# Strassen operand sums of the gate and FFN stages formed in earlier stages and kept in DRAM, one plain pair less in each stage, in a hybrid mixer layer on one core

## The chip, the core and the metric

The kernel runs on one core of a Trainium2 chip. A core has a matrix engine (TensorE, here PE), a vector engine (VectorE, DVE), a scalar engine (ScalarE, ACT), a general engine (GpSimd, POOL), a sync engine (SyncE, SP) that issues most of the transfers, and 16 DMA engines that move data between device memory (DRAM) and the on-chip memory (SBUF); matmul results land in a second on-chip memory, PSUM. Each engine runs its own instructions strictly in program order and waits for others by semaphores. The metric is the device time of one execution in microseconds (us), the median of several runs.

## The reference

One layer (batch 1, 1024 tokens, width 1024, all float32). Cut to what matters here:

```python
u = rms_norm(x, norm_mix_pre)
z = u @ w_in                       # split into the inputs of three branches and gate_pre
y_gla, y_s5, y_ml = ...            # gated linear attention, S5 scan, mLSTM; each projected to width 1024
gates = sigmoid(gate_pre).reshape(1, 1024, 3, 1024)
merged = gates[:, :, 0] * y_gla + gates[:, :, 1] * y_s5 + gates[:, :, 2] * y_ml
x = x + rms_norm(merged @ w_out, norm_mix_post)
u = rms_norm(x, norm_ffn_pre)
a = causal_dwconv(u @ w_up, conv_w, conv_b)            # 2816 channels, 3 taps
x = x + rms_norm((gelu(a) * (u @ w_gate)) @ w_down, norm_ffn_post)
```

## The kernel before, in words

**Matmuls.** Every float32 operand is held as two fp32r tiles, a rounded one ("hi") and the rest ("lo"), and a product is made of three matmuls: hi·hi, hi·lo, lo·hi. `split(hi, lo, src)` (L88, L89) makes the two: a copy on ACT, then a subtraction on DVE.

**Stages in order of time.** Normalisation and transposes of x and the value projections (0 to 84 us); the projection `su` of the S5 branch (`su_half`, 84 to 135 us), during which DVE, ACT and POOL prepare the gates and decays of the first heads and the S5 tables; the heads of the three branches (to 579 us); the 24 gate tiles in 12 pairs (to 823 us); the branch projections (to 975 us); the output projection with both norms (to about 1080 us); the 22 FFN channel blocks f (to 1500 us); the down projection.

**Order of work.** The order on every engine is the order in which the program issues instructions. In the first stages preparatory work is written as generators, called turns: `spawn(gen, wait)` registers one, `tick(us)`, called in the middle and at the end of each 128-token matmul tile (`tok_mm`, L229 and the eviction to `ev`, L243), advances a modelled clock and resumes up to two turns that are due. Turns of the `su` stage are the GLA gate turn (L384 to L398 make the cumulative decay `g`), the mLSTM gate turn (L517 to L527, whose last DVE step L524 feeds the matmul L527), and the S5 turn (a chain of small POOL multiplies and sums, L680 to L686 and L776, that make the tables `ptab` and `gtab`, which DVE reads at L835 and L817).

**Gate and FFN stages.** The transposed input of a stage is held in four tiles (`uk`, and `ub` for the FFN): halves of the contraction `kh` by halves of the tokens `n`. A pair of weight tiles is multiplied either plainly (`std`, 96 matmuls 128x512) or by a Strassen scheme (`run`, 84 matmuls, L1061), which needs four combined input operands t0 to t3, themselves sums of the quarters, split in hi and lo. `combos(k)` forms a quarter of them in SBUF on DVE (whole values L1023, sums L1029 to L1032, then `split`). In the gate stage the plain pair 0 runs before the operand tiles exist and the plain pairs 1 and 2 run while `combos` fill them (two calls in each, GSTD = 2); in the FFN the blocks 0, 1, 2 are plain (NSTD = 3) and `combos` are called after blocks 0 and 1. `prep` splits the weights of a Strassen pair on ACT and DVE and forms weight sums on POOL (L1047 to L1050).

**Around the start of the FFN.** The output projection handles eight token blocks i. Each is squared and summed on ACT (L1346), scaled on DVE (L1348), added to x (L1349), and a delayed closure `post` squares again (L1354), scales (L1356, writing `xr`), and transposes on PE (L219) into the FFN's input tiles `u200..u211`, which two splits fill. The FFN's block 0 is run in two halves of the tokens, so that its first half can run before block i = 7 is transposed. `conv` (L1385 on ACT, L1387 twice on DVE) reads a block's up result from PSUM, and L1401 multiplies by its gate result; PSUM holds two such results (`z`), so the first matmuls of block f = 1 wait for the second L1387 of block 0.

Of the kernel before, what the change touches and what calls it, by code (L numbers as in the profile page):

```python
# [18 lines left out]
S = 1024  # L19
# [13 lines left out]
def hybrid_layer(ctx: ExitStack, tc: tile.TileContext, a, out, dbg=None):  # L33
# [132 lines left out]
    def spawn(gen, wait=0.0):  # L166
        turns.append([now[0] + wait, gen])
        return turns[-1]
# [11 lines left out]
    def flat(ps):  # L180
        return ps.rearrange("p a b -> p (a b)")

    GSTD = 2

    MVB = 0
    v_dram = [dram.tile([8, 128, W], F32, name=f"v{b}") for b in range(2)]
    su_dram = dram.tile([8, 128, W], F32, name="su")
# [27 lines left out]
    def transpose_split(src, hi_of, lo_of, first=None):  # L215
        for hf in range(2):
            ps = bank([128, 4, 128])
            for k in range(4):
                ins = pe.transpose(ps[:, k, :], src[:, (hf * 4 + k) * 128:(hf * 4 + k + 1) * 128], ident)  # L219
                if first is not None:  # L220
                    after(first, ins)
            split(hi_of(hf), lo_of(hf), ps)

    def tok_mm(wt, i, lhs, put, c0, to=None):
        hi, lo = wt
# [696 lines left out]
    def s5_all():  # L922
        s5_base()
        yield 20.0
        for s in range(8):
# [2 lines left out]
            yield from s5_set(s)  # L928
            yield 2.5

    def su_half(hf):
        wt = wide_tile(w_in, C_SU + hf * 256, 256)
        for i in range(8):
            tok_mm(wt, i, tok_lhs, put_dram(su_dram), hf * 256)
            if i == 1 and hf == 0:
                gates.append(spawn(gla_gates(0, E)))
                spawn(ml_gates(), 10.0)
        su_done.append(hf)
# [3 lines left out]
    gates = []  # L942
    E = []
    spawn(s5_all())
    su_half(0)
    su_half(1)

# [60 lines left out]
    def f32v(t):  # L1008
        return t.bitcast(F32)

    def strassen(stack, base, spare):
        tpl = stack.enter_context(tc.tile_pool(name="st", bufs=1, reuse_waits="tile"))
        xp = stack.enter_context(tc.tile_pool(name="sx", bufs=1, reuse_waits="tile"))
        tp = stack.enter_context(tc.tile_pool(name="sc", bufs=2, reuse_waits="tile"))
        ut = [tuple(tpl.tile([128, 4, 512], F32R, name=f"t{i}{q}") for q in "hl") for i in range(4)]

        def combos(k):
            e = xp.tile([128, 3, 512], F32, tag="xh", name="xh")
            d = xp.tile([128, 3, 512], F32, tag="xl", name="xl")

            def whole(dst, kh, n):
                hi, lo = base(kh, n)
                dve.tensor_tensor(dst, f32v(hi)[:, k, :], f32v(lo)[:, k, :], op=ALU.add)  # L1023

            whole(e[:, 0], 0, 0)
            whole(e[:, 1], 0, 1)
            whole(e[:, 2], 1, 1)
            whole(d[:, 1], 1, 0)
            dve.tensor_tensor(d[:, 0], e[:, 2], e[:, 1], op=ALU.subtract)  # L1029
            dve.tensor_tensor(e[:, 1], e[:, 1], e[:, 0], op=ALU.subtract)  # L1030
            dve.tensor_tensor(e[:, 0], d[:, 0], e[:, 0], op=ALU.add)
            dve.tensor_tensor(d[:, 1], d[:, 1], e[:, 0], op=ALU.subtract)  # L1032
            for i, src in enumerate((e[:, 1], e[:, 0], d[:, 0], d[:, 1])):
                split(ut[i][0][:, k, :], ut[i][1][:, k, :], src)

        def prep(raw, swap):
            ah = wpool.tile([128, 4, 512], F32R, tag="hi", name="hi")
            al = wpool.tile([128, 4, 512], F32R, tag="lo", name="lo")
            if swap:
                bh, bl = spare  # L1040
            else:
                bh = xp.tile([128, 3, 512], F32R, tag="xh", name="xh")
                bl = xp.tile([128, 3, 512], F32R, tag="xl", name="xl")
            a11, a12, a21, a22 = (merge(raw[:, i, k:k + 4]) for i in range(2) for k in (0, 4))
            for i, src in ((0, a11), (1, a12), (2, a22)):
                split(ah[:, i], al[:, i], src)
            pool.tensor_tensor(a22, a21, a22, op=ALU.add)  # L1047
            pool.tensor_tensor(a21, a11, a21, op=ALU.subtract)
            pool.tensor_tensor(a11, a22, a11, op=ALU.subtract)
            pool.tensor_tensor(a12, a12, a11, op=ALU.subtract)  # L1050
            split(ah[:, 3], al[:, 3], a11)
            for i, src in ((0, a22), (1, a21), (2, a12)):
                split(bh[:, i], bl[:, i], src)
            return (ah, al), (bh, bl)

        def prod(ps, w, i, b):
            (hi, lo), (bh, bl) = w, b
            for k in range(4):
                c = slice(k * 128, (k + 1) * 128)
                for p, (l, r) in enumerate(((hi, bh), (hi, bl), (lo, bh))):  # L1060
                    pe.matmul(ps, l[:, i, c], r[:, k, :], start=(k == 0 and p == 0), stop=(k == 3 and p == 2))  # L1061
            return ps

        def plus(o, x, y):
            return dve.tensor_tensor(o, x, y, op=ALU.add)  # L1065

        def run(w):
            wa, wb = w
            za, zb = big(), big()
            u = tp.tile([128, S], F32, tag="u", name="u")  # L1070
            gt = tp.tile([128, S], F32, tag="gt", name="gt")
            u0, u1, g0, g1 = u[:, 0:512], u[:, 512:], gt[:, 0:512], gt[:, 512:]
            p1, p2 = prod(za[:, 0, :], wa, 0, base(0, 0)), prod(za[:, 1, :], wa, 1, base(1, 0))
            act.copy(g0, p1)
            plus(u0, g0, p2)
            p6, p5 = prod(zb[:, 0, :], wa, 3, ut[1]), prod(zb[:, 1, :], wb, 0, ut[0])
            mark = plus(g0, g0, p6)
            plus(u1, g0, p5)
            plus(g0, g0, prod(bank([128, 512]), wb, 1, ut[2]))
            plus(g1, g0, p5)  # L1080
            mark3 = plus(u1, u1, prod(bank([128, 512]), wb, 2, base(1, 1)))
            mark4 = plus(g0, g0, prod(bank([128, 512]), wa, 2, ut[3]))
            return u, gt, (mark, mark3), (mark3, mark4)

        return combos, prep, run, tp

    def gate_raw(b, jj):
        c0 = C_G + b * D + jj * 256
# [2 lines left out]
            sync.dma_start(raw[:, i], w_in[:, c0 + i * 128:c0 + (i + 1) * 128].rearrange("(k p) c -> p k c", p=128))  # L1091
        return raw

    def prep_std(raw):
        hi = wpool.tile([128, 2, 8, 128], F32R, tag="hi", name="hi")
        lo = wpool.tile([128, 2, 8, 128], F32R, tag="lo", name="lo")
        for i in range(2):
            split(hi[:, i], lo[:, i], raw[:, i])
        return hi, lo

    def std(w, e, ns=(0, 1), ps=None):
# [24 lines left out]
    def u_base(kh, n):  # L1126
        return tuple(t[:, :, n * 512:(n + 1) * 512] for t in uk[kh])

    combos, prep, run, tp = strassen(gstack, u_base, None)
    done = 0  # L1130
    while gpairs:
        b, jj = gpairs.pop(0)
        raw = gate_raw(*gpairs[0]) if gpairs else None
        if isinstance(w[0], tuple):
            nw = prep(raw, False) if gpairs else None
            u, gt, _, last_adds = run(w)
            srcs = dsts = (u, gt)
        else:
            for k in range(done, done + 4 // GSTD):
                combos(k)  # L1140
            done += 4 // GSTD
            nw = prep_std(raw) if done < 4 else prep(raw, False)
            srcs = [flat(std(w, e)) for e in range(2)]
            dsts = [tp.tile([128, S], F32, tag=t, name=t) for t in ("u", "gt")]
        last_tanhs = [put_gate(gate_dram[b][jj * 2 + e], dsts[e], srcs[e]) for e in range(2)]
        w = nw
# [90 lines left out]
        parts[nh, kh] = [split(hi[:, k, :], lo[:, k, :], raws[k // 2][:, k % 2, :]) for k in range(4)]  # L1237
        wo[nh, kh] = (hi, lo)

    last_m = []  # L1240
    def project(b, os_):
        wp = a[("gla_w_proj", "s5_w_proj", "ml_w_proj")[b]][0]
        chain[0] = b == 0
# [2 lines left out]
        for j in range(8):  # L1246
# [34 lines left out]
    u2p = ffn1.enter_context(tc.tile_pool(name="u2", bufs=1, reuse_waits="tile"))  # L1281
    ub = {(kh, n): tuple(u2p.tile([128, 4, 512], F32R, name=f"u2{kh}{n}{q}") for q in "hl")
          for kh in range(2) for n in range(2)}
    with tc.tile_pool(name="dt", bufs=2, reuse_waits="tile") as dt, tc.tile_pool(name="dx", bufs=2, reuse_waits="tile") as dx, tc.tile_pool(name="dy", bufs=2, reuse_waits="tile") as dy, tc.tile_pool(name="wo", bufs=1, reuse_waits="tile") as wop:
        ms = {}

        def load_m(i):
# [43 lines left out]
        for i in range(8):  # L1331
# [17 lines left out]
            dve.tensor_tensor(x1, x1, xr, op=ALU.add)  # L1349
            sync.dma_start(x1_dram[i], x1)  # L1350

            def post(first=None, x1=x1, xr=xr, ts=ts):
                ssq = small.tile([128, 1], F32, tag="ssq", name="ssq")
                act.activation(xr, x1, AF.Square, accum_out=ssq)  # L1354
                r = rstd_of(ssq, 1, D)
                dve.scalar_tensor_tensor(out=xr, in0=x1, scalar=r[:, 0:1], in1=gpre, op0=ALU.mult, op1=ALU.mult)  # L1356
                n, c = ts.start // 512, slice(ts.start % 512, ts.start % 512 + 128)
                transpose_split(xr, lambda hf: ub[hf, n][0][:, :, c],
                                lambda hf: ub[hf, n][1][:, :, c], first)

            pend.append(post)
        flush()
# [6 lines left out]

    w_up, w_gt, w_dn = a["ffn_w_up"][0], a["ffn_w_gate"][0], a["ffn_w_down"][0]  # L1370
    h_dram = [dram.tile([128, S], F32, name=f"h{f}") for f in range(NF)]
    NSTD = 3
    xs = (v_hi, v_lo)
    combos, prep, run, tp = strassen(ffn1, lambda kh, n: ub[kh, n], ub[0, 1])

    def f_raw(f):
        fc = slice(f * 128, (f + 1) * 128)
# [28 lines left out]
    for f in range(NF):  # L1406
        nw = None
        if f + 1 < NF:
            nw = prep_std(f_raw(f + 1)) if f + 1 < NSTD else prep(f_raw(f + 1), (f + 1 - NSTD) % 2)
        if f < NSTD:  # L1410
            zs = [big(), big()]
            for ns in (((0,), (1,)) if f == 0 else ((0, 1),)):
# [6 lines left out]
            lastc.append(mark)  # L1419
        w = nw  # L1420
        if f < NSTD - 1:
            for k in (2 * f, 2 * f + 1):
                combos(k)
    ffn1.close()

    tail.clear()
# [234 lines left out]
```

## Time and profile before

| | |
|---|---|
| median of 3 runs | 1723.81 us (1723.78 to 1723.91) |
| profiled execution | 1727.5 us, span of its instructions 1725.8 us |
| mean granted TensorE clock | 0.995 of full speed |
| PE busy | 1686.1 us, 98% of the span |
| DVE busy | 1183.8 us (69%) |
| ACT busy | 669.2 us (39%) |
| POOL busy | 257.1 us (15%) |
| moved by DMA | 193.01 MB, mean 112 GB/s |

A profile is one execution. "Busy" is the time in which an engine had at least one instruction in work. Idle time of an engine is put down to what released it ("<-DVE xr" means that the last thing it waited for was the DVE instruction that wrote `xr`). Times in the views count from the span's start.

### The profile page before, as it was taken

The page shows a single profiled execution, that of the slowest core. Times are in us where ns is not written, and L with a number is a line of the kernel's source. Part 1 is how long each engine was busy: PE and PEld are TensorE (multiplying, and loading weights), DVE is VectorE, ACT ScalarE, POOL GpSimd, SP SyncE. Part 2 cuts the span into 40 slices and gives each one's busy share as a digit, 9 for nine tenths or more (in the row PEclk, how much of TensorE's full clock was granted, in tenths as well). Part 3 has the DMA queues.
Part 4 walks back from the last instruction along what each step waited for, and adds up shares of the span by engine and source line. Part 5 has one row for each costly group of instructions (what it writes and reads, how often), then busy time and mean ns, then how long its engine had stood idle before and what let it go on. Part 6 is the DMA issues. An engine that isn't in the chain of part 4 may idle for free. (4 is left out here: it accounts for less than half of the span.)

```text
span 1725.8 us, 21824 instructions
## 1 busy us (share of the span) xinstructions
PE 1686.1 (98%) x8492; PEld 1412.8 (82%) x8492; DVE 1183.8 (69%) x1607; ACT 669.2 (39%) x1012; POOL 257.1 (15%) x327
## 2 busy tenths in 40 slices
PE   6999999999999999999999999999999999999997
PEld 6998778898888888888888887888888888888886
DVE  3456679757788484445735655967777777679987
ACT  4453464444444133333500333433333333244343
POOL 1140000010000012222000011033223322101021
PEclk9999999999999999999999999999999999999999
DMA  6233032333223223335655633222322222573161
GB/s 205 66 98 83 7 101 70 82 105 95 57 74 93 81 73 122 103 98 190 237 171 184 206 122 120 64 74 73 91 81 86 73 89 83 193 277 116 57 224 49
DMA packets 195624, 193.01 MB, mean 112 GB/s; under 512 B 29159, under 2 KB 154256, under 8 KB 195520
## 3 DMA queue, kind: packets, MB, share of 16 engines
q1 hardware_dynamic: 194352, 187.41, 34.7%
q0 software_dynamic: 1168, 4.19, 0.7%
q8 instruction: 67, 1.10, 0.3%
q14 instruction: 37, 0.30, 0.1%
HBM read 141.22 MB, written 48.25 MB: 110 GB/s over the span
## 5 line engine op out<-in xcount | busy, mean ns | idle before, releaser
L89 DVE TENSOR_TENSOR lo<-raw,hi 128x512 fp32r<-128x512 f32 (+2 forms) x184 | 174.2, 968 | 115.3 <-ACT hi L88 112.5
L88 ACT CAST hi<-raw 128x512 fp32r<-128x512 f32 (+2 forms) x184 | 132.0, 751 | 291.3 <-PE z L130 154.3
L130 PE MATMUL z<-ohl,hi 128*128 128x512 f32 x448 | 121.1, 392 | 0.0
L1047 POOL TENSOR_TENSOR raw<-raw 128x512 f32<-128x512 f32 x28 | 39.5, 1410 | 486.9 <-DVE lo L89 398.2
L130 PEld LDWEIGHTS z<-ohl,hi 128*128 128x128 f32 x448 | 84.3, 188 | 18.9
L130 PE MATMUL z<-u1h,hi 128*128 128x512 f32 x240 | 79.2, 410 | 0.0
L130 PE MATMUL z<-u0h,hi 128*128 128x512 f32 x240 | 78.0, 406 | 0.0
L130 PE MATMUL z<-u1l,hi 128*128 128x512 f32 x240 | 75.3, 393 | 0.0
L130 PE MATMUL z<-u0l,hi 128*128 128x512 f32 x240 | 75.3, 394 | 0.0
L130 PE MATMUL z<-u0h,lo 128*128 128x512 f32 x240 | 75.0, 393 | 0.0
L130 PE MATMUL z<-u1h,lo 128*128 128x512 f32 x240 | 74.9, 393 | 0.0
L130 PE MATMUL z<-ohl,lo 128*128 128x512 f32 x224 | 69.5, 392 | 0.0
L1387 DVE SCALAR_TENSOR_TENSOR cv<-u,fcol,cv 128x1023 f32<-128x1023 f32 (+1 forms) x38 | 48.7, 1281 | 24.0 <-ACT cv L1385 24.0
L68 POOL TENSOR_SCALAR rstd<-ssq 128x1 f32<-128x1 f32 (+1 forms) x32 | 7.9, 246 | 375.8 <-ACT x L1346 246.9
L229 PE MATMUL z<-hi,u0h 128*128 128x256 f32 (+1 forms) x188 | 55.8, 302 | 6.3 <-ACT u0h L88 3.6
L89 DVE TENSOR_TENSOR xl<-raw,xh 128x512 fp32r<-128x512 f32 x57 | 51.8, 935 | 11.7 <-ACT xh L88 8.8
L1385 ACT ACTIVATE cv<-u,fcol 128x1024 f32<-128x1024 f32 x19 | 23.7, 1247 | 89.8 <-DVE u L1065 89.8
L229 PE MATMUL z<-hi,u0l 128*128 128x256 f32 (+1 forms) x188 | 55.0, 293 | 0.5 <-DVE u0l L89 0.3
L229 PE MATMUL z<-hi,u1h 128*128 128x256 f32 (+1 forms) x188 | 55.0, 293 | 0.0
L229 PE MATMUL z<-lo,u0h 128*128 128x256 f32 (+1 forms) x188 | 54.5, 291 | 0.0
L229 PE MATMUL z<-lo,u1h 128*128 128x256 f32 (+1 forms) x188 | 54.0, 287 | 0.0
L229 PE MATMUL z<-hi,u1l 128*128 128x256 f32 (+1 forms) x188 | 53.9, 287 | 0.0
(563 smaller groups left out, 4877.6 us busy)
## 6 DMA issues: line engine op xcount, KB each, us to landing
raw<-in_w_in_dram SPq DMA_DIRECT2D x48, 512.0 KB, 5.3
pt<-gate SPq DMA_DIRECT2D x24, 512.0 KB, 5.3
raw<-in_ffn_w_up_dram SPq DMA_DIRECT2D x22, 512.0 KB, 4.1
raw<-in_ffn_w_gate_dram SPq DMA_DIRECT2D x22, 512.0 KB, 5.9
h<-cv SPq DMA_DIRECT2D x21, 512.0 KB, 2.6
bx<-in_ffn_w_down_dram SPq DMA_DIRECT2D x15, 512.0 KB, 4.2
by<-in_ffn_w_down_dram SPq DMA_DIRECT2D x15, 512.0 KB, 6.7
gate<-u SPq DMA_DIRECT2D x11, 512.0 KB, 3.0
```

What stands on the lines that cost most here:

```text
L68: pool.tensor_scalar(r, ssq, 1.0 / width, EPS, op0=ALU.mult, op1=ALU.add)
L88: made = (ordered("act", act.copy(hi, src)), ordered("dve", dve.tensor_tensor(lo, src, hi.bitcast(F32), op=ALU.subtract)))
L89: ordered("dve", dve.tensor_tensor(lo, src, hi.bitcast(F32), op=ALU.subtract)))
L130: pe.matmul(ps[:, n, :], l[:, k, c], r(k, n), start=(k == 0 and p == 0), stop=(k == nk - 1 and p == 2))
L229: pe.matmul(ps, lhs(l, k, i), r[:, k, :], start=(k == 0 and p == 0), stop=(k == 7 and p == 2))
L1047: pool.tensor_tensor(a22, a21, a22, op=ALU.add)
L1385: first = act.activation(cv, src, AF.Identity, scale=fcol[:, 44 + f:45 + f], bias=fcol[:, 66 + f:67 + f])
L1387: ins = dve.scalar_tensor_tensor(out=cv[:, k:], in0=src[:, 0:S - k], scalar=fcol[:, (2 - k) * 22 + f:(2 - k) * 22 + f + 1], in1=cv[:, k:], ...
```

## The change

Three parts. In the gate stage, the sums behind the operands t0 to t3 are formed during the `su` stage by a new turn `mixed`, written to four DRAM tensors `tg`, read back by `fill` at the start of the gate stage, and split by `settle`; pair 2 becomes a Strassen pair and the `combos` of that stage go. In the FFN, the sums for the first half of the columns are formed in `post` of token blocks 4 and 5, written to DRAM tensors `t2` and read back; the other half is formed by two `combos` calls, now by column blocks, ahead of block 0's `conv`; block 2 becomes a Strassen block. The casts of block f = 1's weights are ordered behind the splits of the last transposes (`last_post`).

```diff
-    GSTD = 2
@@
-            split(hi_of(hf), lo_of(hf), ps)
+            made = split(hi_of(hf), lo_of(hf), ps)
+        return made
@@
+    tg_dram = [dram.tile([128, 4, 512], F32, name=f"tg{i}") for i in range(4)]
+
+    def sums(e, d):
+        dve.tensor_tensor(d[1], d[1], e[1], op=ALU.subtract)
+        dve.tensor_tensor(e[1], e[1], e[0], op=ALU.subtract)
+        dve.tensor_tensor(e[0], d[1], e[0], op=ALU.add)
+        dve.tensor_tensor(d[0], d[0], e[0], op=ALU.subtract)
+        return e[1], e[0], d[1], d[0]
+
+    def mixed():
+        for k in range(4):
+            ts = [g([128, S]) for _ in range(2)]
+            for t, (hi, lo) in zip(ts, uk):
+                dve.tensor_tensor(t, hi[:, k, :].bitcast(F32), lo[:, k, :].bitcast(F32), op=ALU.add)
+            yield 1.5
+            made = sums(*([t[:, 0:512], t[:, 512:]] for t in ts))
+            for i in range(4):
+                sync.dma_start(tg_dram[i][:, k, :], made[i])
+            yield 3.0
@@
     spawn(s5_all())
+    spawn(mixed(), 3.0)
     su_half(0)
@@
+        def fill(t_dram, c):
+            for i in (1, 0, 2, 3):
+                sync.dma_start(f32v(ut[i][1])[:, :, c], t_dram[i][:, :, c])
+
+        def settle(i, c=slice(0, 512), ks=(slice(0, 2), slice(2, 4))):
+            for k in ks:
+                split(ut[i][0][:, k, c], ut[i][1][:, k, c], f32v(ut[i][1])[:, k, c])
+
+        def combos(pair):
+            c = slice(pair * 128, (pair + 1) * 128)
+            ts = []
+            for kh, tag in enumerate(("xh", "xl")):
+                t = xp.tile([128, 3, 512], F32, tag=tag, name=tag)
+                ts.append([t[:, n].rearrange("p (k c) -> p k c", k=4) for n in range(2)])
+            for i, src in enumerate(pair_sums(base, c, *ts)):
+                split(ut[i][0][:, :, c], ut[i][1][:, :, c], src)
@@
-    def prep_std(raw):
+    def prep_std(raw, since=None):
...
-            split(hi[:, i], lo[:, i], raw[:, i])
+            made = split(hi[:, i], lo[:, i], raw[:, i])
+            for first, then in zip(since or (), made):
+                after(first, then)
@@
-    done = 0
+    fill(tg_dram, slice(0, 512))
     while gpairs:
...
-            for k in range(done, done + 4 // GSTD):
-                combos(k)
-            done += 4 // GSTD
-            nw = prep_std(raw) if done < 4 else prep(raw, False)
+            settle(1)
+            settle(0)
+            nw = prep(raw, False)
+            settle(2)
+            settle(3)
@@
+                last_post[:] = transpose_split(xr, lambda hf: ub[hf, n][0][:, :, c],
+                                               lambda hf: ub[hf, n][1][:, :, c], first)
+                if i in (4, 5):
+                    ts_ = [mx.tile([128, 2, 4, 128], F32, tag=t, name=t) for t in ("me", "md")]
+                    made = pair_sums(lambda kh, n: ub[kh, n], c, *([t[:, 0], t[:, 1]] for t in ts_))
+                    for j in range(4):
+                        sync.dma_start(t2_dram[j][:, :, c], made[j])
@@
-    NSTD = 3
+    NSTD = 2
@@
-            nw = prep_std(f_raw(f + 1)) if f + 1 < NSTD else prep(f_raw(f + 1), (f + 1 - NSTD) % 2)
+            if f + 1 < NSTD:
+                nw = prep_std(f_raw(f + 1), last_post)
+                fill(t2_dram, slice(0, 256))
+                combos(2)
+                combos(3)
+            else:
+                nw = prep(f_raw(f + 1), (f + 1 - NSTD) % 2)
@@
         if f < NSTD - 1:
-            for k in (2 * f, 2 * f + 1):
-                combos(k)
+            for i in (1, 0, 2, 3):
+                settle(i, slice(0, 256), (slice(0, 4),))
```

`pair_sums` makes the four whole values (L1035 of the changed kernel) and then calls `sums` (L933 to L936 there). Lines of the changed kernel are one lower than before from L229 to L835, and then higher: L1348, L1356, L1387 and L1401 of before are L1378, L1386, L1422 and L1436 there.

Three places show how the instructions now stand. The first is DVE in the `su` stage, from the S5 turn's reciprocal to the mLSTM gate turn's last step (L524 before, L523 after) that PE's L527 (L526) needs. Before:

```order
L747 RECIPROCAL q_920<-q_920 128x32
L806 TENSOR_SCALAR q_1263<-iob,t_hi 128x128
L738 TENSOR_SCALAR q_920<-q_920 128x32
...
L389 TENSOR_TENSOR g<-g 128x1024
L390 SCALAR_TENSOR_TENSOR g<-cmask,g 128x1024
L517 TENSOR_TENSOR g<-lif,bf 128x8x4
L392 TENSOR_TENSOR g<-g 128x1024
L517 TENSOR_TENSOR g<-lif,bi 128x8x4
L519 SCALAR_TENSOR_TENSOR g<-g 128x32
L523 TENSOR_SCALAR g<-g 128x32
L524 TENSOR_TENSOR g<-g 128x32
```

The last part of the same stretch in the changed kernel (L943 are the whole values of `mixed`, L933 to L936 its sums):

```order
L943 TENSOR_TENSOR g<-u0h,u0l 128x1024
L943 TENSOR_TENSOR g<-u1h,u1l 128x1024
L388 TENSOR_TENSOR g<-g 128x1024
...
L518 SCALAR_TENSOR_TENSOR g<-g 128x32
L933 TENSOR_TENSOR g<-g 128x512
L834 TENSOR_TENSOR ca<-ca,ptab 128x4x128
L934 TENSOR_TENSOR g<-g 128x512
L89 TENSOR_TENSOR lo<-raw,hi 128x1024
L935 TENSOR_TENSOR g<-g 128x512
L936 TENSOR_TENSOR g<-g 128x512
L943 TENSOR_TENSOR g<-u0h,u0l 128x1024
L943 TENSOR_TENSOR g<-u1h,u1l 128x1024
L522 TENSOR_SCALAR g<-g 128x32
L523 TENSOR_TENSOR g<-g 128x32
```

Eight L943 and twelve L933 to L936, two weight splits (L89) and the S5 step L834, which before came after L524, now stand ahead of L523. On PE, L526 stands 40 matmuls later than L527 did.

The second place is DVE during FFN block 0, from the last scaling of `xr` to the second tap of block 0's `conv`. Before:

```order
L1356 SCALAR_TENSOR_TENSOR xr<-x_8819,rstd,gpre 128x1024
L1023 TENSOR_TENSOR xh<-u200h,u200l 128x512
L1023 TENSOR_TENSOR xl<-u210h,u210l 128x512
L89 TENSOR_TENSOR u201l<-m,u201h 128x4x128
L89 TENSOR_TENSOR u211l<-m,u211h 128x4x128
...
L1387 SCALAR_TENSOR_TENSOR cv<-z,fcol,cv 128x1023
L1023 TENSOR_TENSOR xh<-u211h,u211l 128x512
L1387 SCALAR_TENSOR_TENSOR cv<-z,fcol,cv 128x1022
```

In the changed kernel:

```order
L89 TENSOR_TENSOR lo<-raw,hi 128x1024 x2
L1035 TENSOR_TENSOR xl<-u211h,u211l 128x512
L89 TENSOR_TENSOR t1l<-t1l,t1h 128x4x256
L933 TENSOR_TENSOR xl<-xl,xh 128x512
L89 TENSOR_TENSOR t0l<-t0l,t0h 128x4x256
...
L1035 TENSOR_TENSOR xl<-u210h,u210l 128x512
L1035 TENSOR_TENSOR xl<-u211h,u211l 128x512
L1422 SCALAR_TENSOR_TENSOR cv<-z,fcol,cv 128x1023
L933 TENSOR_TENSOR xl<-xl,xh 128x512
L1422 SCALAR_TENSOR_TENSOR cv<-z,fcol,cv 128x1022
```

Between the last L1386 and the second L1422 there are 25 DVE instructions; before there were 18 between L1356 and the second L1387. The added ones are the two weight splits of f = 1 and the settling of t0, t1 and t2 (each 128x1024).

The third place is ACT at the last two token blocks. Before, the two casts of f = 1's weights (`hi<-raw`) stand one ahead of and one behind the squares of block i = 7 (L1346) and of i = 6 (L1354):

```order
L88 CAST hi<-raw 128x1024
L1346 ACTIVATE x_8819,ssq<-z 128x1024
L1354 ACTIVATE xr,ssq<-x_8731 128x1024
L88 CAST hi<-raw 128x1024
L88 CAST u201h<-m 128x4x128
```

In the changed kernel they stand behind the last transposes' casts:

```order
L1376 ACTIVATE x_8869,ssq<-z 128x1024
L1384 ACTIVATE xr,ssq<-x_8767 128x1024
L88 CAST u201h<-m 128x4x128
L88 CAST u211h<-m 128x4x128
L1384 ACTIVATE xr,ssq<-x_8869 128x1024
L88 CAST u201h<-m 128x4x128
L88 CAST u211h<-m 128x4x128
L88 CAST hi<-raw 128x1024 x2
```

## Rows read from the trace of the kernel before

**Rows 1.** The page's busy times of each engine.
```profile
PE 1686.1 (98%) x8492; PEld 1412.8 (82%) x8492; DVE 1183.8 (69%) x1607; ACT 669.2 (39%) x1012; POOL 257.1 (15%) x327
```
**Rows 2.** PE's waits: line waited for, total us, times, longest.
```profile
PE m L219 <- DVE xr L1356: 3.0, 1, 3.0
PE z L229 <- ACT ev L243: 2.4, 2, 1.6
```
**Rows 3.** PE timeline, plain FFN block 0 (start, duration, instruction).
```profile
1089.70 0.39 PE L130 MATMUL z<-u201h,lo 128*128 128x512 f32 x1
...
1094.01 0.40 PE L130 MATMUL z<-u200h,hi 128*128 128x512 f32 x1
```
**Rows 4.** SP timeline at the start of the gate stage.
```profile
602.42 0.32 SPq L1106 DMA_DIRECT2D gate<-g  x1
```
**Rows 5.** Windows: length, busy of each engine, PEclk, DMA share, GB/s.
```profile
810.00:815.00 5.00, 5.00 (x23) 4.14 (x23) 3.62 (x6) 2.10 (x3) 1.09 (x2) 1.00 1.03 401
```
**Rows 6.** ACT timeline, token blocks 5 to 7 (in brackets: idle before, releaser).
```profile
1042.06 1.03 ACT L1346 ACTIVATE x<-z 128x1024 f32<-128x1024 f32 x1 [4.83 <-PE z L1308]
...
1053.92 1.03 ACT L1346 ACTIVATE x<-z 128x1024 f32<-128x1024 f32 x1 [4.83 <-PE z L1308]
...
1067.96 1.05 ACT L88 CAST hi<-raw 128x1024 fp32r<-128x1024 f32 x1 [7.01 <-DMA raw<-in_ffn_w_up_dram]
1068.92 1.02 ACT L1346 ACTIVATE x<-z 128x1024 f32<-128x1024 f32 x1
```
**Rows 7.** PE timeline at the transposes of block 6.
```profile
1070.12 0.39 PE L130 MATMUL z<-u210h,lo 128*128 128x512 f32 x1
1073.53 1.09 PE L219 MATMUL m<-ident,xr 128*128 128x128 f32 x8 [3.02 <-DVE xr L1356]
...
1074.78 0.63 PE L130 MATMUL z<-u210l,hi 128*128 128x512 f32 x1
...
1078.10 0.40 PE L130 MATMUL z<-u200h,hi 128*128 128x512 f32 x1
```
**Rows 8.** DVE timeline, FFN block 0.
```profile
1077.29 1.28 DVE L1356 SCALAR_TENSOR_TENSOR xr<-x,rstd,gpre 128x1024 f32<-128x1024 f32 x1 [0.35 <-POOL rstd L69]
1078.49 0.69 DVE L1023 TENSOR_TENSOR xh<-u200h,u200l 128x512 f32<-128x512 f32 x1
1079.09 0.69 DVE L1023 TENSOR_TENSOR xl<-u210h,u210l 128x512 f32<-128x512 f32 x1
1081.21 0.69 DVE L89 TENSOR_TENSOR u201l<-m,u201h 128x512 fp32r<-128x512 f32 x1 [1.43 <-ACT u201h L88]
...
1091.85 1.28 DVE L1387 SCALAR_TENSOR_TENSOR cv<-z,fcol,cv 128x1022 f32<-128x1022 f32 x1
1093.04 0.68 DVE L1023 TENSOR_TENSOR xl<-u210h,u210l 128x512 f32<-128x512 f32 x1
```
**Rows 9.** DVE timeline, su stage.
```profile
95.88 1.22 DVE L389 TENSOR_TENSOR g<-g 128x1024 f32<-128x1024 f32 x1 [3.34 <-ACT g L387]
...
105.98 0.19 DVE L524 TENSOR_TENSOR g<-g 128x32 f32<-128x32 f32 x1 [2.96 <-ACT g L521]
```
**Rows 10.** PE timeline, su stage.
```profile
112.40 0.28 PE L229 MATMUL z<-lo,u1h 128*128 128x256 f32 x1
112.52 0.30 PE L527 MATMUL m<-g,triu 128*128 128x32 f32 x2
```
**Rows 11.** POOL timeline, su stage and Strassen weight sums of the gates.
```profile
89.09 0.46 POOL L680 TENSOR_TENSOR q<-ptab,q 128x32 f32<-128x32 f32 x2
...
100.07 1.54 POOL L683 TENSOR_TENSOR ptab<-ptab,q 128x128 f32<-128x128 f32 x1
...
632.74 4.62 POOL L1047 TENSOR_TENSOR raw<-raw 128x512 f32<-128x512 f32 x1 [88.68 <-ACT t2h L88]
637.44 1.30 POOL L1048 TENSOR_TENSOR raw<-raw 128x512 f32<-128x512 f32 x1
```
**Rows 12.** DVE timeline, last of the gate stage's combos before an idle.
```profile
635.51 0.70 DVE L89 TENSOR_TENSOR t1l<-xh,t1h 128x512 fp32r<-128x512 f32 x1
```

## What the change is expected to do

> **What bounds the kernel now.** I read the page's busy times first: PE works 98% of the span [rows 1], so time is won by taking matmuls away or by removing a wait of PE, and lost by a new wait; work added to DVE (69%), ACT (39%) or POOL (15%) costs nothing until PE waits for it. PE's waits come next [rows 2]. Behind those at the program's start, which the change doesn't touch, the largest are 3.0 us for one `xr` of L1356 at the start of the FFN and 2.4 us for evictions of the `su` stage; both lie where the change puts new work. So I went through the change stage by stage and asked each time when PE reaches an instruction and when its operand is ready.
>
> **Matmuls taken away.** A plain pair is 96 matmuls of 128x512 and a Strassen pair 84. One pair changes kind in each of two stages: 24 matmuls. In the plain block 0 of the FFN, 19 matmuls take from 1089.70 to 1094.01, 0.227 us each [rows 3]; so 12 are 2.7 us, in the gates and again in the FFN.
>
> **Gate stage: -2.7.** What was formed by `combos` is now read back: `fill` stands on SP behind the store of pair 0, issued at 602.42 [rows 4]. It reads four tensors of 1.05 MB. In another stretch of this stage the DMA engines moved 401 GB/s [rows 5]; at that speed the 4.2 MB are there about 10.5 us later, near 613. The Strassen run of pair 2 can begin when plain pair 1 ends: pair 0 ended some 1.5 us ahead of its store, and 96 x 0.227 = 21.8 later it is 622.7. The run needs its first combined operand some 5.5 us later (24 matmuls of plain quarters come first). The splits of `settle` (eight on ACT and eight on DVE) fit between, because DVE loses the combos, whose last instruction ended at 636.2 [rows 12]. That is a margin of about 15 us, so I cost this at nothing; if it were gone (loads at under 170 GB/s), PE would wait for t1. Bounds: -2.7 and, with late loads, +3.
>
> **FFN, the cast moved away: -3.4 at the start of block 0's second half.** ACT squared token blocks 5 and 6 at 1042.06 and 1053.92, 11.86 us apart; block 7's square would follow at about 1065.8, but it ran at 1068.92, behind a cast of f = 1's weights that had waited 7.01 us for its load [rows 6]. All that follows shifted with it: `xr` of block 6 was late, PE waited 3.02 us, and afterwards ran at half clock: matmul starts were 0.415 us apart from 1074.78 to 1078.10 (8 of them) where 0.227 is full speed [rows 7], about 1.7 us more over some nine matmuls. With the cast behind the last splits, block 7's square can run near 1065.8. The sums of `post` for token block 5 then sit on DVE between 1065.4 and 1067.8 and hold back POOL's `rstd`, so that I put `xr` of block 6 at 1071.1 and that of block 7, which began at 1077.29 [rows 8], at 1075.4. PE would still stand about 0.8 and 0.7 us for them. The second half of block 0 would begin 3.4 us earlier than before.
>
> **FFN, DVE behind it: +6.4.** PE's first matmul of f = 1 needs the PSUM tile that block 0's second `conv` tap reads. Before, DVE got from the last L1356 (1077.29) to the end of that tap at 1093.04, and PE started f = 1 at 1094.01 without a wait [rows 3, 8]. Now DVE has 25 instructions there. Small two-input operations of 128x512 start 0.60 us apart (1078.49 to 1079.09), and the tap takes 1.19 (1091.85 to 1093.04) [rows 8]; one of 128x1024 is taken as twice the small one less its overhead, 1.14. Eight whole values 4.8, two splits of the last transposes 1.2, two weight splits 2.3, three settles 3.4, five sums 3.0, four splits of combined operands 2.4, two taps 2.4: 19.5 us. Before the last splits DVE stood 1.43 us for ACT [rows 8]; with one more whole value ahead of it, 0.9 is left. From the end of L1386 at 1076.6 the tap ends near 1097.0. PE is through block 0 at 1094.0 - 3.4 = 1090.6, so it waits some 6.4 us there, and f = 1 begins 3.0 us later than before. A wait of 3.02 us was followed by half clock [rows 7]; I count the same 1.7 us here. So FFN: +3.0 + 1.7 - 2.7 = **+2.0**. Bounds: if DVE's queue kept up, the stage would gain 3.4 + 2.7 = 6.1; if another 2 us of DVE work or waits fell into it, +4.
>
> **su stage: +3.3.** `mixed` puts eight whole values (128x1024, 1.22 us each [rows 9]) and twelve sums (0.60) ahead of L523: 9.8 + 7.2 us; two weight splits and the S5 step L834 now stand ahead of it too, 2.9. That is 19.9 us in a queue that had idle times of 3.34 and 2.96 before L389 and L524 [rows 9]. L524 began at 105.98, so L523 would come near 105.98 + 19.9 - 6.3 = 119.6. PE ran L527 at 112.52, with matmuls 0.12 apart before it [rows 10]; it is 40 matmuls later in the order, 4.8, so PE arrives near 117.3 and waits 2.5 us. Behind L526 on PE stand the rest of `su` and the heads, which make it up nowhere. Lower bound 0.4, if DVE also fills smaller gaps, some 2 us in all, between its instructions of 89 to 106. The eviction wait of 2.4 us [rows 2] comes from ACT standing for DVE and I expect it to stay about as long.
>
> The upper bound is POOL's. Its small S5 operations run 0.2 to 0.5 us each, but a weight sum that takes 1.30 us at 637.44 took 4.62 us from 632.74, to 637.36, while DVE ran two-input operations in SBUF back to back until 636.2 [rows 11, 12]: it got nothing done until DVE stood still. From 89.09 to 100.07 POOL makes `ptab` [rows 11], 28 operations, some 8.3 us of work with each at its unstretched time, and L834 waits for it. If all of it had to run while DVE waits, L523 would be later by up to 5.5 us: 8. But DVE also runs operations from PSUM and one-input ones there, beside which POOL went on. I take 0.8 of it, near the lower end, and keep 0.4 and 8.
>
> The Trainium skill ("SBUF — State Buffer", Who interferes with whom) says that a DVE instruction with two SBUF inputs contends with a GpSimd instruction that reads SBUF, and that in the contended modes whoever issues first holds the shared ports for the whole instruction while the other blocks. The row at 632.74 agrees. By that rule alone the upper part of the bound would apply, about 6 us in this stage instead of 3.3.
>
> **Sum.** -2.7 + 2.0 + 3.3 = +2.6 us. Against the profiled execution of 1727.5 that is 1730.1; the median of the runs shown is 3.7 lower, and I carry the difference to it: 1723.81 + 2.6 = **1726.4**. A measurement of this kernel can tell about 0.2%, 3.4 us, from no change (1720.4 to 1727.3).
>
> **The rivals.**
> - *The DVE work is hidden (faster, 0.20).* For it: DVE is busy 69%, and the wait for `xr` with its slow clock is a real loss of 4.7. Against it: the list of 25 instructions ahead of the tap. The gates give -2.7, the FFN -6.1, the su stage +2: -6.8, 1717.0. It decides if f = 1 starts before 1094.
> - *POOL is locked out in the su stage (slower, 0.33).* The place is L834's wait for `ptab`; the row at 632.74 speaks for it, the PSUM and one-input work between against it. L523 comes near 124: +6.5, and a clock loss like the one above, 1.5: -2.7 + 2.0 + 8.0 = +7.3, 1731.1. It decides from about 4.2 us lost in this stage on.
> - *The read-back is late (slower, 0.04).* If `fill` were to take 28 us (150 GB/s), PE would wait about 5 us for t1 and its splits: 1731.
> - *As forecast (0.43):* a saving in each of the two stages eaten by the two new waits, its own range 1721 to 1728.
>
> Faster 0.20, within 0.2% 0.43, slower 0.37. The range 1718 to 1732 runs from near the first rival to just past the second and third, and leaves out cases below and above them with about 1 in 10 each.
>
> **What would show it.** PE with 24 matmuls less and no wait for t0 to t3 in the gates; no wait of 3.0 us for `xr` (two under 1 us); a wait of L130 for DVE `cv` L1422 of 4 to 8 us at the start of f = 1 with half clock behind it; a wait of L526 for L523 of 2 to 6 us near 117; POOL's L680 stretched between 89 and 115. The prediction is wrong if the waits for L1422 or L523 are missing, if an eviction of `su` waits longer than 3 us, or if t1 is late in the gates.

## The result

The changed kernel is slower. Its median is 1741.22 us (four runs, 1738.07 to 1743.53) beside 1723.86 us for the kernel before (1723.78 to 1724.91): a ratio of 1.0091, 95% interval 1.0079 to 1.0103, +15.7 us (the two medians differ by 17.4). The prediction said 1726.4, with 1732 as its upper end. The profiled execution took 1738.07 us, the shortest of the four:

```profile
core 0: 1736.3 us, clock 0.993
```

Five landmarks on PE cut both traces into stretches: the first 128x256 matmul of `su`, the first transposes of the S5 output (L914 of before, L913 after), the first projection matmul, the last matmul with t3 in the FFN, and the last matmul of all. Lengths in us, worked out from the start times:

| stretch | before | after | difference |
|---|---|---|---|
| start to `su` | 79.45 | 76.33 | -3.1 |
| `su` to the S5 transposes | 143.67 | 150.78 | +7.1 |
| to the first projection | 594.65 | 591.37 | -3.3 |
| to the end of the FFN | 685.11 | 685.89 | +0.8 |
| to the last matmul | 212.91 | 222.54 | +9.6 |

The first stretch holds nothing that the change touches; it is taken up at the end. The five differences add up to +11.1, less than the medians tell: the profiled execution of the changed kernel was its shortest, and that of before took 1727.5 us, 3.7 more than its median. PE's waits in the changed kernel (line waited for, total us, times, longest), which answer to [rows 2]:

```profile
PE q L1560 <- ACT hi L88: 7.7, 1, 7.7
PE z L130 <- DVE cv L1422: 4.6, 1, 4.6
PE z L228 <- ACT ev L242: 3.9, 3, 2.1
...
PE m L526 <- DVE g L523: 1.7, 1, 1.7
PE m L217 <- DVE xr L1386: 1.5, 2, 0.9
```

Four of the five rows are those the prediction spoke of. The largest, 7.7 us, is at the first matmul of the down projection, of which it said nothing.

**su stage.** PE's timeline of the changed kernel, answering to [rows 10]:

```profile
113.88 0.58 PE L228 MATMUL z<-hi,u0h 128*128 128x256 f32 x1 [2.13 <-ACT ev L242]
...
117.04 0.40 PE L228 MATMUL z<-lo,u1h 128*128 128x256 f32 x1
117.25 0.31 PE L228 MATMUL z<-hi,u1h 128*128 128x256 f32 x1
119.29 0.41 PE L526 MATMUL m<-g,triu 128*128 128x32 f32 x2 [1.73 <-DVE g L523]
```

and the windows of the same stretch (PE, PEld, DVE, ACT, POOL busy, then granted clock, DMA share, GB/s):

```profile
100.00:112.00 12.00, 11.02 (x89) 10.40 (x87) 11.96 (x12) 7.51 (x12) 11.84 (x9) 1.00 0.31 99
112.00:118.00 6.00, 3.68 (x16) 3.47 (x16) 5.96 (x7) 2.07 (x5) 3.94 (x5) 0.72 0.53 143
118.00:124.00 6.00, 4.71 (x27) 4.60 (x28) 5.76 (x16) 0.37 (x1) 0.00 (x0) 0.73 1.13 304
```

Matmuls start 0.21 apart from 114.26 to 117.25, right behind the wait at 113.88, where 0.12 is full speed [rows 10]. Behind the wait at 119.29 they run at 0.12 at first and 0.21 apart from 120.71 to 123.91, 16 matmuls each time: half clock twice. DVE is the engine that never rests (11.96 of 12 us). Its timeline, answering to [rows 9], and POOL's, to [rows 11]:

```profile
111.15 1.23 DVE L834 TENSOR_TENSOR ca<-ca,ptab 128x512 f32<-128x512 f32 x1
...
119.05 0.19 DVE L523 TENSOR_TENSOR g<-g 128x32 f32<-128x32 f32 x1
```

```profile
104.57 2.44 POOL L682 TENSOR_TENSOR ptab<-ptab,q 128x128 f32<-128x128 f32 x1
106.97 1.81 POOL L679 TENSOR_TENSOR gtab<-ptab,q 128x256 f32<-128x256 f32 x1
```

**Start of the FFN.** PE's timeline, answering to [rows 7], and DVE's, to [rows 8]:

```profile
1071.93 1.09 PE L217 MATMUL m<-ident,xr 128*128 128x128 f32 x8 [0.94 <-DVE xr L1386]
...
1077.03 1.09 PE L217 MATMUL m<-ident,xr 128*128 128x128 f32 x8 [0.56 <-DVE xr L1386]
...
1096.62 0.50 PE L130 MATMUL z<-u200h,hi 128*128 128x512 f32 x1 [4.64 <-DVE cv L1422]
```

```profile
1075.69 1.28 DVE L1386 SCALAR_TENSOR_TENSOR xr<-x,rstd,gpre 128x1024 f32<-128x1024 f32 x1 [1.16 <-POOL rstd L69]
...
1095.19 1.28 DVE L1422 SCALAR_TENSOR_TENSOR cv<-z,fcol,cv 128x1022 f32<-128x1022 f32 x1
```

The wait of 3.0 us for `xr` is now two of 0.94 and 0.56, and block f = 1 waits 4.64 us for the second tap.

**Start of the down projection.** PE's last matmuls on the weight sums of FFN block 21 and the first of the down projection, in the changed kernel:

```profile
1501.57 0.40 PE L1086 MATMUL m<-u211h,u201l 128*128 128x512 f32 x1
...
1512.51 0.80 PE L1560 MATMUL q<-hi 128*128 128x512 f32 x1 [7.74 <-ACT hi L88]
```

before:

```profile
1500.08 0.40 PE L1061 MATMUL m<-u211h,xl 128*128 128x512 f32 x1
```

The loads of the first tiles of the down projection, `aa` from `h`, on POOL's and SP's queue, in the changed kernel:

```profile
1502.27 1.18 POOL L1490 DMA_DIRECT2D aa<-h  x2 [24.29 <-PE m L1086]
```

```profile
1490.71 0.38 SPq L1495 DMA_DIRECT2D bx<-in_ffn_w_down_dram  x1
1502.00 0.79 SPq L1490 DMA_DIRECT2D aa<-h  x2
```

and POOL's and SP's before:

```profile
1481.52 1.18 POOL L1449 DMA_DIRECT2D aa<-h  x2 [5.02 <-PE m L1061]
```

```profile
1489.23 0.38 SPq L1454 DMA_DIRECT2D bx<-in_ffn_w_down_dram  x1
1489.66 1.36 SPq L1449 DMA_DIRECT2D aa<-h  x2
```

The second operand of the matmul at the end of block 21 was `xl` before and is `u201l` now. `prep(raw, swap)` puts the second half of a Strassen pair's weights into `xh`, `xl` or, every other block, into `u201`, an input tile that Strassen blocks don't read; which one is `(f + 1 - NSTD) % 2`. With NSTD one lower every block changed sides, and the last one came to stand in `u201`. The down projection's `aa0` and `aa2` get the place of `u201` in SBUF. Before, block 20 was its last user, and the loads went out at 1481.52 (POOL) and 1489.66 (SP). Now it is block 21, which reads it until 1501.97, and the loads go out at 1502.27 (POOL, 21 us later) and 1502.00 (SP, 12 us later), with SP's later loads queued behind.

### The profile page after: what moved, and what is told of

It reads as the page before. It is cut to its first block, busy times and chain, and to the rows that moved or that the text cites. A ratio compares the mean times of both kernels' runs of the same rounds, so it can differ in the third digit from the quotient of the medians.

```text
span 1736.3 us, 21882 instructions
## 1 busy us (share of the span) xinstructions
PE 1683.8 (97%) x8468; PEld 1409.4 (81%) x8468; DVE 1200.8 (69%) x1611; ACT 671.1 (39%) x1012; POOL 278.9 (16%) x335
## 4 chain that ended last, share of the span: by engine, by line
PE 84%; DVE 9%; ACT 2%; DMA 2%; issue 1%; POOL 1%; SPq 0%; DVEq 0%; POOLq 0%; ACTq 0%
PE z L130 25%; PE z L1086 19%; PE m L1086 14%; PE z L1338 5%; PE m L1560 5%; PE z L228 4%; PE z L1560 4%; PE q L1560 2%; DVE lo L89 2%; DVE q L883 1%; PE m L434 1%; DVE q L893 0%; PE q L869 0%; DMA aa<-h 0%; PE m L650 0%
## 5 line engine op out<-in xcount | busy, mean ns | idle before, releaser
L89 DVE TENSOR_TENSOR lo<-raw,hi 128x512 fp32r<-128x512 f32 (+2 forms) x188 | 176.2, 960 | 113.9 <-ACT hi L88 111.0
L130 PE MATMUL z<-u1h,hi 128*128 128x512 f32 x224 | 74.3, 411 | 0.0
L130 PE MATMUL z<-u0h,hi 128*128 128x512 f32 x224 | 73.5, 409 | 0.0
L130 PE MATMUL z<-u0l,hi 128*128 128x512 f32 x224 | 70.7, 396 | 0.0
L130 PE MATMUL z<-u0h,lo 128*128 128x512 f32 x224 | 70.5, 394 | 0.0
L130 PE MATMUL z<-u1l,hi 128*128 128x512 f32 x224 | 70.3, 393 | 0.0
L130 PE MATMUL z<-u1h,lo 128*128 128x512 f32 x224 | 69.8, 393 | 0.0
L1422 DVE SCALAR_TENSOR_TENSOR cv<-u,fcol,cv 128x1023 f32<-128x1023 f32 (+1 forms) x40 | 51.2, 1280 | 25.0 <-ACT cv L1420 25.0
L89 DVE TENSOR_TENSOR xl<-raw,xh 128x512 fp32r<-128x512 f32 x60 | 54.3, 932 | 13.1 <-ACT xh L88 10.4
L1090 DVE TENSOR_TENSOR u<-gt,z 128x512 f32<-128x512 f32 x60 | 41.1, 684 | 18.5 <-ACT gt L1099 17.7
```

Source lines behind the costliest of these rows:

```text
L89: ordered("dve", dve.tensor_tensor(lo, src, hi.bitcast(F32), op=ALU.subtract)))
L130: pe.matmul(ps[:, n, :], l[:, k, c], r(k, n), start=(k == 0 and p == 0), stop=(k == nk - 1 and p == 2))
L1422: ins = dve.scalar_tensor_tensor(out=cv[:, k:], in0=src[:, 0:S - k], scalar=fcol[:, (2 - k) * 22 + f:(2 - k) * 22 + f + 1], in1=cv[:, k:], ...
```

## The experiments

All were timed in five rounds beside the kernel before on the same chip; ratios are to that kernel, whose runs lay between 1723 and 1730 us. In the diffs, a line that starts with `#`, or a remark behind one, tells in words what is longer in the code. The theory after the result: +7 in the `su` stage (DVE's queue, the evictions and the half clock behind the waits), -3 in the gates, about +1 in the FFN, +10 at the down projection by the place of `u201`. The rival for the last: the loads are late because of the added transfers or their queue.

**place.** Only the addresses of the down projection's tiles change; the order of instructions on every engine stays.

```diff
-    bx, a11, a12, by, a21 = (block(n) for n in ("bx", "aa", "ab", "by", "ac"))
+    # tiles one by one: bx0 aa0 bx2 aa2 (where u200 was), ac0 ac2 ac5 ac7 (u201),
+    # bx4 aa4 bx5 aa5 bx7 (u210), then the rest
```

> The changed kernel with one edit: the tiles of the down projection are placed so that bx0, aa0, bx2, aa2 (needed first) lie where u200 was and bx4 to bx7 where u210 was, and u201 goes to tiles loaded later; the order of instructions on every engine is that of the changed kernel. Theory A (u201 is held by the last FFN block's second weight part because its parity flipped, so the loads into its place wait for that block's last use): the 7.7 us wait for ACT hi and some 3 us of half clock behind it go, 1741.2 - 10.5 = about 1730.7 us. Rival B (the loads are late because of the added transfers or the queue, not the place): no change, 1741.

Measured: 1732.05 us, 1.0035 (1.0023 to 1.0047); the changed kernel had 1.0091. The `hi` wait is gone: the first matmul of the down projection follows with no wait, and SP's load of `aa` went out at 1497.75, 13 us ahead of the last matmul with t3 (1510.98 in this run), where the changed kernel has 2 us (1502.00, 1504.37). PE and SP of this run:

```profile
1511.21 0.40 PE L1564 MATMUL q<-hi 128*128 128x512 f32 x1
```

```profile
1497.32 0.38 SPq L1499 DMA_DIRECT2D bx<-in_ffn_w_down_dram  x1
1497.75 1.67 SPq L1494 DMA_DIRECT2D aa<-h  x2
```

The stretch to the last matmul is 213.45 us (before 212.91, changed 222.54).

**before_late.** The same lever on the kernel before, the other way.

```diff
-    bx, a11, a12, by, a21 = (block(n) for n in ("bx", "aa", "ab", "by", "ac"))
+    # order of the tiles: bx, ab, by0, aa, the rest of by, ac: aa0 and aa2 where u211h was
```

> The kernel before with one edit: aa0 and aa2 are placed where u211 was, which the last FFN block reads until about 3 us before its end; the order of instructions is that of before. Theory A: PE waits some 7 to 8 us at the start of the down projection, half clock behind it, +10 us: about 1734 us. Rival B: a place costs nothing, 1723.9.

Measured: 1735.5 us, 1.0055 (1.0043 to 1.0068). The kernel before, with nothing but addresses changed, loses as much. Its SP and PE:

```profile
1487.49 0.38 SPq L1457 DMA_DIRECT2D bx<-in_ffn_w_down_dram  x1
1498.78 0.80 SPq L1452 DMA_DIRECT2D aa<-h  x2
```

```profile
1508.38 0.79 PE L1522 MATMUL q<-hi 128*128 128x512 f32 x1 [6.84 <-ACT hi L88]
```

The last stretch is 222.61 us. Together the two runs settle the cause; the rival falls, since neither changes a transfer or the order of any engine.

**gates_only and ffn_only.** Each part of the change alone.

```diff
 # gates_only
-                if i in (4, 5):
+                if i in ():
-    NSTD = 2
+    NSTD = 3          # combos by k after blocks 0 and 1, casts of block 1, as before
 # ffn_only
-    spawn(mixed(), 3.0)
-    fill(tg_dram, slice(0, 512))
+    # combos by k in plain pairs 1 and 2, as before
```

> Only the gate part of the change: mixed in the su stage, read-back, GSTD gone; FFN as before. By the two profiles: su stage +7 (1.7 for L523, 1.5 more for evictions, about 3.7 of half clock), gates -2.7: +4.3, about 1728 us. Rival (the extra su loss is chance of that one profile, as the prediction's 3.3): +0.6, 1724.5.

> Only the FFN part: t2, NSTD 2, casts behind the last splits; su and gate stage as before. Theory A: FFN -1.4 and the down projection +10.5, about 1733 us. Rival B (the down loss needs the gates' added transfers, or is from them in part): below 1727.

Measured: gates_only 1730.68 us, 1.0029 (1.0020 to 1.0038), its `su` stretch 151.84 us and that to the projection 593.31; ffn_only 1735.53 us, 1.0055 (1.0042 to 1.0068), with the last stretch at 221.03. Waits of PE in the two:

```profile
PE z L228 <- ACT ev L242: 3.9, 3, 2.2
...
PE m L526 <- DVE g L523: 2.5, 1, 2.5
```

```profile
PE q L1577 <- ACT hi L88: 5.1, 1, 5.1
PE z L130 <- DVE cv L1439: 4.6, 1, 4.6
```

The two parts, +5.0 and +9.8 us, come near the whole (14.8 of 15.7). Each part alone is a loss, the FFN part by the place of `u201`.

**casts.** The third part alone, on the kernel before.

```diff
-            nw = prep_std(f_raw(f + 1)) if f + 1 < NSTD else prep(...)
+            nw = prep_std(f_raw(f + 1), last_post if f == 0 else None) if f + 1 < NSTD else prep(...)
```

> The kernel before with one part of the change: the casts of block 1's weights ordered behind the splits of the last transposes. If the wait of 3.0 us for xr and the half clock behind it (1.7) come from that cast: both go, two waits under 1 us stay, and DVE reaches block 0's second tap about 1 to 1.5 us after PE is through: about -3 us, 0.998 of before. Rival (the wait only moves to the tap, as in the changed kernel): a wait of 3 us or more there and 1.000.

Measured: 1722.96 us, 0.9985 (0.9976 to 0.9994), -2.6 us. The wait for `xr`, with no wait for the tap:

```profile
PE m L219 <- DVE xr L1359: 1.1, 2, 0.6
```

**mixlate, convfirst, best.** Three repairs on `place`: the sums of `mixed` made later, in the mLSTM value projection; `settle` and the last `combos` ordered behind block 0's second tap; both.

```diff
 # mixlate
-    spawn(mixed(), 3.0)              # at the start of su
+    spawn(mixed(), 3.0)              # ahead of the loop with C_MV
 # convfirst
-                combos(3)            # with the casts of block 1
+                settle(i, slice(0, 256), (slice(0, 4),), tap[0])   # its DVE part after the tap
+            combos(3, tap[0])
 # best: mixlate and convfirst
```

> The run 'place' with one edit more: mixed is spawned at the start of the mLSTM value projection instead of at the start of the su stage. If mixed in the su stage costs what the profiles show (7 to 8.6 us from the start of su to the first S5 output transposes): about -7.5 us against 'place', 1724.5. Rival (its DVE work stops PE wherever it stands): 1729 or more, with new waits of PE for DVE between 340 and 400 us.

> The run 'place' with one edit more: settle and the last combos call of the FFN are ordered behind block 0's second tap. If block 1's wait of 4.6 us and the half clock behind it (1.7) come from DVE's queue ahead of that tap: about -5.5 us against 'place', 1726.5, with a wait under 1 us there. Rival (the operands t0 to t3 are then late for block 2): a wait of L1086 for DVE or ACT of 3 us or more near 1115, 1730.

> place, mixlate and convfirst together. If the three losses are independent: 1732 - 7.5 - 5.5 = 1719, 0.996 of before, of which 5.4 are the 24 matmuls less and the rest the xr wait and its clock. Rival (some of the two gains is lost to new waits): 1723 to 1726, no faster than before.

Measured: mixlate 1728.39 us, 1.0015 (1.0006 to 1.0024), -3.7 against `place`, half of what was expected. Its `su` stretch is back at 143.24 us, but a new wait stands in the value projection:

```profile
380.59 0.39 PE L228 MATMUL z<-hi,u0h 128*128 128x256 f32 x1 [2.79 <-ACT ev L242]
```

convfirst 1725.48 us, 1.0004 (0.9995 to 1.0013), -6.6 against `place`; no wait for the tap is among the waits, nor one for t0 to t3. best 1721.11 us, 0.9968 (0.9956 to 0.9981): faster than before, with an eviction wait of 2.63 us left at 379.72.

**mixsu, spread, heads.** Where `mixed` may stand, each on `place` with `convfirst`.

```diff
 # mixsu: the same su stage, 30 us of the turns' clock later
-    spawn(mixed(), 3.0)
+    spawn(mixed(), 33.0)
 # spread: best, with 12 us between the steps of mixed
-            yield 3.0
+            yield 12.0
 # heads: spawned at the second mLSTM head instead
+        if h == 1:
+            spawn(mixed(), 3.0)
```

> The run 'convfirst' with mixed spawned 30 us of the turns' clock later in the same su stage, so that its first DVE step stands behind L523 and the S5 tables. If the su loss is its place ahead of L523 and of POOL's chain: most of the 7 to 8 us goes, 1719. Rival (its 34 us of DVE work are too much for this part of the kernel): L526's wait goes, others take its place, 1723 or more.

> The run 'best' with 12 instead of 3 us of the turns' clock between the four steps of mixed. If the eviction wait of 2.6 us at 380 in 'best' comes from the density of DVE work: it goes, about 1718.5. Rival (one step's adds at that place are enough): 1721.

> The run 'best' with mixed spawned at the second mLSTM head, where no eviction stands behind it. If only its place counts: no eviction wait at 380, about 1718.5 us. Rival (DVE is as full there, and the waits for DVE g of L628 and L617 grow): 1721 or more.

Measured: mixsu 1717.91 us, 0.9954 (0.9940 to 0.9968); spread 1718.81 us, 0.9965 (0.9953 to 0.9978); heads 1729.59 us, 1.0021 (1.0012 to 1.0030). In mixsu the `su` stretch is 143.31 us, as long as before, with all of `mixed` in it; the waits of PE there and DVE's first step of `mixed`:

```profile
PE z L228 <- ACT ev L242: 2.1, 2, 1.3
```

```profile
114.64 1.22 DVE L943 TENSOR_TENSOR g<-u0h,u0l 128x1024 f32<-128x1024 f32 x1
```

In spread the wait at 380 is gone, as expected, but the run changes more than the spacing: its page counts 8480 matmuls where best and mixsu have 8468. The gate stage runs plain pairs as long as a turn is left (`while turns`), and with the longer steps one more pair ran plainly: `gate<-g` is stored four times there and twice in best. By the forecast's price of a pair, 2.7 us, its 1718.81 would be about 1716 (an estimate); that it met the 1718.5 expected is in part chance.

The first theory for heads failed by 11 us. The rival's time (1721 or more) holds, but not its lines: PE stands for DVE at another one,

```profile
481.37 0.76 PE L130 MATMUL z<-u0h,hi 128*128 128x512 f32 x1 [8.84 <-DVE g L586]
```

because a step of an mLSTM head that PE needs at once (L586) stands on DVE behind sums of `mixed` and two weight splits.

## Why the prediction was wrong

**The step that failed: the sum ends at the start of the FFN, and the down projection behind it is put at nothing.** The working went through the change stage by stage and costed the lower NSTD as 12 matmuls less. It left out that NSTD also sets the parity of `swap`, 19 blocks further on, and gave no reason why nothing behind the FFN should change. That is +9.6 of the difference, shown from both sides by `place` and `before_late`. Without it the changed kernel has 1.0035, about 1732 us by those runs, +6 where +2.6 was forecast. The row that would have told it stands in the order of instructions, where the last block reads `u201` in place of `xl`, and in the trace of before, where the load into that place waits for PE until 1481.52.

**su stage: the wait near its forecast, the loss mis-sized.** The stage lost 7.1 us in this profile, 8.7 in place and 8.2 in gates_only, for +3.3. The wait for L523 was 1.73 us (2.6 in place, 2.5 in gates_only) for 2.5, but both of its ends came later than forecast. The two profiles reach `su` 3.1 us apart, so count from its start: L523 was put at 40.2 (119.6 less 79.45) and ran at 42.7; PE was put at L526 at 37.9 and came at 41.2. That the two errors cancel is luck.

PE came late by terms that were mis-sized. The eviction wait, forecast to stay at 2.4, grew to 3.9. And half clock, which the text counted in the FFN, was left out here: 32 matmuls 0.21 apart in place of 0.12 are about 3.0 us. In gates_only the granted clock was 0.50 all the way from 116.2 to 126.2. These, with the wait of 1.7, are 6.2 of the 7.1. Most of the rest is a third stretch at half clock, outside the `su` stage, behind a wait that before has too:

```profile
180.82 2.06 PE L434 MATMUL m<-g 64*128 64x128 f32 x16 [1.51 <-DVE g L425]
182.80 1.22 PE L130 MATMUL z<-u0h,hi 128*128 128x512 f32 x2
```

before:

```profile
176.84 1.77 PE L435 MATMUL m<-g 64*128 64x128 f32 x16 [1.52 <-DVE g L426]
178.54 0.73 PE L130 MATMUL z<-u0h,hi 128*128 128x512 f32 x2
```

It is about 1.5 us, less a wait of 1.0 that is gone behind it; ffn_only, without `mixed`, shows it as well, so that it is not shown to be the change's.

L523 came late because DVE's own instructions were longer than priced. From the reciprocal to L523 DVE took 33.7 us (17.2 before), 16.4 more, where 13.6 was forecast. Five instructions beside POOL's tables (one each of L391, L834, L934, L89 and L943) took 7.4 us, and 5.0 in before or in mixsu away from them. So POOL did cost DVE something, but not by the second rival's mechanism: `ptab` was complete at 107.0 while L834 ran at 111.15, so DVE did not wait for the table. That the stage's loss is near that rival's 8.0 is no proof of it.

That the place of the sums decides, and not the amount of work, is shown by mixsu: the same sums, some 19 us of DVE work (eight of 1.22 and sixteen of 0.60; the expectation put them too high), cost nothing there that the stretch shows. In mixsu they stand behind L523 (104.21) and also behind POOL's tables (done at 104.2), so the run does not part the queue ahead of L523 from the slowing beside POOL.

**Gates: right.** -3.3 in the profile, -1.3 in gates_only, -2.1 in place and -3.2 in convfirst, for -2.7, with no wait for the combined operands. The read-back was not late.

**FFN: right.** +0.8 in the profile, +1.4 in ffn_only and +2.1 in place, for +2.0. PE's waits for `xr` fell to 0.94 and 0.56 (forecast 0.8 and 0.7). The wait for the tap was 4.64 us, forecast 6.4. The stage stands 0.7 us later in this profile (the square of token block 5 began at 1042.77, and at 1042.06 before), so by the forecast's clock the tap ended at 1095.7 and not at 1097.0, and PE was through block 0 some 0.5 later than the 1090.6 forecast. Half clock behind the wait showed from 1096.9 to 1100.3, matmuls 0.43 apart. convfirst shows that DVE's queue ahead of the tap is the cause, and casts that the reordered casts are worth 2.6 us by themselves.

One sentence of the kernel's description needs a limit: an engine's order is not always the written one. `settle` is written behind block 0's `conv` and stands ahead of its taps on DVE; the order shown ahead of the prediction has it there, and it was read as it stood.

## What to carry to other kernels

A count that is changed by one can flip a parity or a rotation of buffers to the end of its loop; look at what the last iteration leaves occupied and which transfer is the first to be placed there. Work moved off a busy stage is free only where no engine soon waits for something queued behind it: the same sums cost 7 to 9 us in the first place, and 3.2 (best) and 11.7 us (heads) more than in mixsu, where they cost nothing to be seen. Count half clock behind each new wait of PE as a risk with a price (here 1.5 us or more each time), not as certain: the same wait had it in one profile and not in another. And before times of two profiles are laid side by side, take off what they differ by at the start of the stage.

## What the runs showed of the hardware

Waits of PE of 2.13, 1.73, 3.02, 4.64 and 7.74 us were each followed by a stretch at half clock, the second after some 1.4 us at full speed, while after waits of 1.61 and 0.81 us in the `su` stage of before, and of 0.94 and 0.56 us for `xr` in the changed kernel, the windows show 1.00. But the length of the wait alone does not tell. In before_late the wait for `xr` that was 3.02 us in before, at the same place, was followed by matmuls 0.23 apart, full speed:

```profile
1073.06 1.09 PE L219 MATMUL m<-ident,xr 128*128 128x128 f32 x8 [2.81 <-DVE xr L1356]
...
1074.69 0.39 PE L130 MATMUL z<-u200h,hi 128*128 128x512 f32 x1
1074.92 0.40 PE L130 MATMUL z<-u200l,hi 128*128 128x512 f32 x1
```

A wait of 2.10 us at 379.10 in place was followed by a granted clock of 1.00 too, and the wait of 1.5 us for L434 (L435 of before) by full clock in before and half clock in the changed kernel. No run here shows what decides between the two.

DVE and POOL slowed each other in the `su` stage: at 104.57 a POOL operation of 128x128 took 2.44 us beside DVE's scan (0.45 in mixsu), and DVE's L834, 128x512, took 1.23 us, and 0.68 in mixsu, where POOL's tables were done. The Trainium skill ("SBUF — State Buffer", Who interferes with whom) has two-input DVE instructions contend with POOL's reads; these rows agree, but POOL went on between DVE's instructions and was not shut out.

The first stretch, the same in all kernels, took 76.33 us in one profile and 79.45 in another, with the granted clock at 1.00 and 0.83 between 20 and 30 us. This is why a difference of 3 us between two single profiles is no evidence here, and why the parts above are read stretch by stretch.
